# An average pooling kernel: stores of two tiles joined into one of 4 MiB, and the last row's store behind the section

## The chip, the cores and the metric

The kernel runs on one core of a Trainium2 chip. The metric is the device time of one execution in microseconds, the median of several runs; lower is better.

## What is computed

`x` has the shape (64, 256, 8192) in float32. Each of its 16,384 rows is cut into windows of four neighbours, and each window gives its mean:

```python
for i in range(out_len):
    start = i * stride            # kernel_size = stride = 4
    output[:, :, i] = np.mean(x[:, :, start : start + kernel_size], axis=2)
```

The output has 16,384 rows of 2,048. So 536.9 MB are read and 134.2 MB are written, and each output element takes three additions and one multiplication.

## The kernel before, in words

The rows are taken 256 at a time. Such a tile has two rows in each of the 128 partitions: 64 KiB per partition, 8 MiB in all, contiguous in memory. There are 64 tiles (`NT`). The input buffer `xin` has room for two of them (`_NIN`), the result buffer `res` for the results of four (`_NOUT`), 2 MiB each.

Four engines' programs are written out by hand inside a critical section (L58), each with its own loop, and tied by semaphores:

- **SP** issues the loads (`load`, L65 to L72). The first two go out at once. Each later one waits on `s_dve` until DVE has finished the tile that held its buffer two tiles earlier. The last tile is loaded as two halves of 4 MiB, one row of each partition each.
- **DVE** (`add_up`, L89 to L101) waits until the store that used the result slot four tiles earlier has landed (`s_out`) and until its tile has landed (`s_in`). It adds neighbours in place (`xin<-xin`, 8192 sums per partition), waits for that, and adds neighbours of the sums into `res` (`res<-xin`, 4096). Then `s_dve` goes up.
- **ACT** multiplies the result by 1/4 in place (`scale` L103, and L141 in the loop) and issues its store of 2 MiB (L143), whose packets have 16 KiB: two output rows of a partition.
- The stores of the last tiles are issued by SP behind its last loads (L119 to L121), except that of the last tile's first half, which ACT issues (L149). A second critical section (L153) waits for the stores.

Each of SP and ACT has a DMA ring of its own. In the profile SP's is q1 and ACT's is q10. A DMA of 128 partitions is cut into one packet per partition, 8 on each of the 16 DMA engines, and a packet of 4 bytes on each engine for the semaphore.

The loop counts: `U = _NOUT` tiles make one turn of a loop, `E = NT // U - 1` turns are in the loops, and the last four tiles are written out behind them.

Of the kernel before, what the change touches and what calls it, by code (L numbers as in the profile page):

```python
# [1 line left out]

# [4 lines left out]

_R = 2  # L10

_NIN = 2
_NOUT = 4


@with_exitstack
def kernel(
    ctx: ExitStack,
    tc: tile.TileContext,
    x: bass.AP,  # L20
    kernel_size: bass.AP,
    stride: bass.AP,
    out: bass.AP,
):
    nc = tc.nc
    K = int(kernel_size)
    assert K == int(stride) == 4
    P = nc.NUM_PARTITIONS
    dt = x.dtype
    inv_k = 1.0 / float(K)  # L30

    xf = x.flatten_outer_dims()
    of = out.flatten_outer_dims()
    rows, L = xf.shape
    OL = of.shape[1]
    R = _R
    T, OT = R * L, R * OL
    assert OL * K == L and rows % (P * R * _NOUT) == 0
    NT = rows // (P * R)

    xg = xf.rearrange("(t p r) m -> p t (r m)", p=P, r=R)
    og = of.rearrange("(t p r) m -> p t (r m)", p=P, r=R)

    pool = ctx.enter_context(tc.tile_pool(name="buf", bufs=1))
    xin = pool.tile([P, _NIN * T], dt)
    res = pool.tile([P, _NOUT * OT], dt)

    s_in = [tc.alloc_semaphore(f"s_in{b}") for b in range(_NIN)]  # L50
    s_out = [tc.alloc_semaphore(f"s_out{b}") for b in range(_NOUT)]
    s_dve = tc.alloc_semaphore("s_dve")
    s_act = tc.alloc_semaphore("s_act")
    s_half = tc.alloc_semaphore("s_half")
    s_last = tc.alloc_semaphore("s_last")
    s_fin = tc.alloc_semaphore("s_fin")

    with tc.tile_critical():  # L58

        U = _NOUT
        E = NT // U - 1

        def load(h, u, r0=0, r1=R, wait=True):  # L65
            b = u % _NIN
            if wait:
                nc.sync.wait_ge(s_dve, h * U + (u - _NIN + 1))
            nc.sync.dma_start(  # L69
                out=xin[:, b * T + r0 * L : b * T + r1 * L],  # L70
                in_=xg[:, h * U + u, r0 * L : r1 * L],
            ).then_inc(s_last if r0 > 0 else s_in[b], 16)  # L72

        def obuf(u, r0=0, r1=R):
            return res[:, u * OT + r0 * OL : u * OT + r1 * OL]

        def store(eng, h, u, r0=0, r1=R, again=False):
            eng.wait_ge(s_act, h * U + (u + 1 + (r1 - 1 if r1 - r0 < R else 0)))
            eng.dma_start(
                out=og[:, h * U + u, r0 * OL : r1 * OL], in_=obuf(u, r0, r1)  # L80
            ).then_inc(s_out[u] if again else s_fin, 16)

        def pairs(out, src):
            v = src.rearrange("p (m k) -> p m k", k=2)
            return nc.vector.tensor_tensor(  # L85
                out=out, in0=v[:, :, 0], in1=v[:, :, 1], op=mybir.AluOpType.add
            )

        def add_up(h, u, r0=0, r1=R):  # L89

            b = u % _NIN
            if r0 > 0:
                nc.vector.wait_ge(s_last, 16)
            else:
                nc.vector.wait_ge(s_out[u], h * 16)
                nc.vector.wait_ge(s_in[b], h * (U // _NIN * 16) + (u // _NIN + 1) * 16)  # L96
            src = xin[:, b * T + r0 * L : b * T + r1 * L]
            half = src[:, : (r1 - r0) * L // 2]
            pairs(half, src).then_inc(s_half, 1)
            nc.vector.wait_ge(s_half, h * U + (u + 1 + (r0 > 0)))  # L100
            pairs(obuf(u, r0, r1), half).then_inc(s_dve, 1)  # L101

        def scale(h, u, r0=0, r1=R):  # L103
            nc.scalar.wait_ge(s_dve, h * U + (u + 1 + (r0 > 0)))
            o = obuf(u, r0, r1)
            nc.scalar.mul(o, o, inv_k).then_inc(s_act, 1)  # L106

        for u in range(_NIN):  # L110
            load(0, u, wait=False)
        with nc.sync.Fori(0, E) as h:
            for u in range(_NIN, U + _NIN):
                load(h, u)
        for u in range(_NIN, U - 1):
            load(E, u)
        for r in range(R):
            load(E, U - 1, r, r + 1, wait=r == 0)
        for u in range(1, U - 1):  # L119
            store(nc.sync, E, u)  # L120
        store(nc.sync, E, U - 1, R - 1, R)  # L121


        with nc.vector.Fori(0, E) as h:
            for u in range(U):
                add_up(h, u)
        for u in range(U - 1):
            add_up(E, u)
        for r in range(R):
            add_up(E, U - 1, r, r + 1)  # L130

        scale(0, 0)
        nc.scalar.wait_ge(s_dve, 2)
        store(nc.scalar, 0, 0, again=True)
        with nc.scalar.Fori(0, E) as h:
            for u in range(1, U + 1):
                v = u % U
                nc.scalar.wait_ge(s_dve, h * U + (u + 1))  # L140
                nc.scalar.mul(obuf(v), obuf(v), inv_k).then_inc(s_act, 1)  # L141
                nc.scalar.wait_ge(s_act, h * U + (u + 1))
                nc.scalar.dma_start(out=og[:, h * U + u, :], in_=obuf(v)).then_inc(  # L143
                    s_out[v], 16
                )
        scale(E, 1)
        scale(E, 2)
        scale(E, 3, 0, 1)
        store(nc.scalar, E, 3, 0, 1)  # L149
        scale(E, 3, 1, 2)  # L150


    with tc.tile_critical():  # L153
        nc.sync.wait_ge(s_out[0], E * 16 + 16)
        nc.sync.wait_ge(s_fin, 64)


# [1 line left out]
_INS = ['x', 'kernel_size', 'stride']  # L159
_OUTS = [((64, 256, 2048), 'float32')]  # L160

_NUMBERS = {'kernel_size': 4, 'stride': 4}


# [26 lines left out]
```

## Time and profile before

| | |
|---|---|
| median of 5 runs | 1555.51 us (1555.32 to 1555.64) |
| profiled execution, its own time | 1555.71 us |
| its span | 1553.9 us |
| DVE busy | 839.8 us, 130 instructions |
| ACT busy | 232.9 us, 66 instructions |
| DMA | 671.10 MB, 18720 packets, mean 432 GB/s |

The span goes from the first to the last instruction of the profiled execution; 1.8 us of its time lie around it. The slices of DMA use on the profile's page are at 90% or more in all 40 slices. Under "waits", DVE waits for loads (702.8 us in 65 waits), ACT for DVE (1312.9 us in 65), and SP for DVE to free a buffer (1462.6 us in 62). Such waits are idle time of an engine; they cost something only where that engine is what the end waits for.

### The profile page before, as it was taken

What the parts mean: (1) busy time and instruction counts of PE and PEld (TensorE: products, weight loads), DVE (VectorE), ACT (ScalarE), POOL (GpSimd) and SP (SyncE); (2) the same over time, 40 slices, a digit from 0 to 9 for tenths busy, and PEclk for the clock granted to TensorE, in tenths of its full rate; (3) what the DMA queues carried; (4) which work ended last, traced back from release to release, by engine and by line L of the source; (5) the groups of instructions that cost most, each with busy time, mean ns of one, the idle gap of its engine ahead of it and who ended that gap; (6) DMA issues with size and microseconds to landing.
All of it is one profiled execution on the core that took longest, in us unless ns stands there. A gap on an engine that the chain in (4) does not pass through costs nothing.

```text
span 1553.9 us, 982 instructions
## 1 busy us (share of the span) xinstructions
DVE 839.8 (54%) x130; ACT 232.9 (15%) x66; POOL 0.2 (0%) x4
## 2 busy tenths in 40 slices
DVE  3645546456464564654646546455464554645546
ACT  1111011110111101111011010110111101111011
POOL 0000000000000000000000000000000000000000
DMA  9999999999999999999999999999999999999999
GB/s 408 420 434 439 439 439 434 420 445 422 439 439 437 434 417 435 437 439 432 442 433 419 434 435 442 439 434 430 424 434 439 439 439 434 423 430 434 439 428 402
DMA packets 18720, 671.10 MB, mean 432 GB/s; under 512 B 2080, under 2 KB 2080, under 8 KB 2080
## 3 DMA queue, kind: packets, MB, share of 16 engines
q1 hardware_dynamic: 9792, 542.12, 80.6%
q10 hardware_dynamic: 8928, 128.98, 19.4%
HBM read 536.87 MB, written 134.22 MB: 432 GB/s over the span
## 4 chain that ended last, share of the span: by engine, by line
DMA 72%; DVE 27%; issue 0%; SPq 0%; ACT 0%; DVEq 0%
DMA xin<-in_x_dram 72%; DVE xin L85 18%; DVE res L85 9%; SPq L69 0%; ACT res L106 0%; DVEq L96 0%; SPq L186 0%; SPq L58 0%
## 5 line engine op out<-in xcount | busy, mean ns | idle before, releaser
L85 DVE TENSOR_TENSOR xin<-xin 128x8192 f32<-128x8192 f32 (+1 forms) x65 | 556.5, 8561 | 702.8 <-DMA xin<-in_x_dram 702.8
L141 ACT ACTIVATE res<-res 128x4096 f32<-128x4096 f32 x60 | 217.0, 3616 | 1226.2 <-DVE res L85 1226.2
L85 DVE TENSOR_TENSOR res<-xin 128x4096 f32<-128x4096 f32 (+1 forms) x65 | 283.4, 4359 | 2.2
L106 ACT ACTIVATE res<-res 128x4096 f32<-128x4096 f32 (+1 forms) x5 | 14.7, 2934 | 86.7 <-DVE res L85 86.7
L106 ACT ACT_TABLE_LOAD x1 | 1.3, 1283 | 0.9 <-SPq L58 0.9
L172 POOL MEMSET const-bfloat16-1.0<- 128x1 bf16 x1 | 0.1, 101 | 0.0
L172 POOL MEMSET const-uint8-127<- 128x1 uint8 x1 | 0.1, 101 | 0.0
L172 POOL MEMSET const-float32-0.0<- 128x1 f32 x1 | 0.1, 98 | 0.2 <-issue 0.2
L172 POOL MEMSET const-float32-1.0<- 128x1 f32 x1 | 0.1, 98 | 0.0
## 6 DMA issues: line engine op xcount, KB each, us to landing
out_dram<-res ACTq DMA_DIRECT2D x61, 2048.0 KB, 52.4
xin<-in_x_dram SPq DMA_DIRECT2D x2, 4096.0 KB, 29.5
out_dram<-res SPq DMA_DIRECT2D x2, 2048.0 KB, 27.1
out_dram<-res ACTq DMA_DIRECT2D x1, 1024.0 KB, 13.1
out_dram<-res SPq DMA_DIRECT2D x1, 1024.0 KB, 5.9
xin<-in_x_dram SPq DMA_DIRECT2D x63, 34.9
```

The source lines that it names most:

```text
L85: return nc.vector.tensor_tensor(out=out, in0=v[:, :, 0], in1=v[:, :, 1], op=mybir.AluOpType.add)
L106: nc.scalar.mul(o, o, inv_k).then_inc(s_act, 1)
L141: nc.scalar.mul(obuf(v), obuf(v), inv_k).then_inc(s_act, 1)
L172: nc = _bacc.Bacc("TRN2", target_bir_lowering=False, num_devices=1)
```

## The change

It has these parts:

- A group of four rows per partition (`_F = 4`) takes the place of the tile as the unit of layout. A tile is still two rows per partition and 8 MiB, but two tiles now make one group of 16 MiB, and a tile's 64 KiB in a partition are half of the 128 KiB that the group has there.
- `res` has two slots of 4 MiB (`_NOUT = 2`), one for each group of results. ACT scales both tiles of a group and then issues one store of 4 MiB with packets of 32 KiB. DVE waits for a slot's store once per group.
- DVE works on a whole tile in four instructions: the pair sums of the first 8,704 inputs in place (4352), their pair sums into `res` (2176), the pair sums of the other 7,680 inputs into a new buffer `hb` (3840, `_B`), and their pair sums into `res` (1920). After the third the input buffer is free, and `s_free`, which loads wait for, goes up there.
- At the end ACT issues no late stores. SP issues, behind its loads, one store of 4 MiB and one of 3 MiB (three of four rows), and behind the critical section, as soon as that is left, the last row's 1 MiB. The section waits for no late store; there is no second section.

Cut to its core:

```diff
-_NOUT = 4
+_F = 4
+_NOUT = 2
+_B = 3840
...
-    og = of.rearrange("(t p r) m -> p t (r m)", p=P, r=R)
+    og = of.rearrange("(g p f) m -> p g (f m)", p=P, f=F)
+    xg = xf.rearrange("(g p f) m -> p g (f m)", p=P, f=F)
...
-    res = pool.tile([P, _NOUT * OT], dt)
+    res = pool.tile([P, _NOUT * F * OL], dt)
+    hb = pool.tile([P, _B], dt)
...
-        U = _NOUT
+        U = _NOUT * G
...
-                nc.sync.wait_ge(s_dve, h * U + (u - _NIN + 1))
+                nc.sync.wait_ge(s_free, h * U + (u - _NIN + 1))
...
+            if u % G == 0 and r0 == 0:
+                nc.vector.wait_ge(s_out[u // G], h * 16)
...
-            pairs(half, src).then_inc(s_half, 1)
+            n = (r1 - r0) * L // 2
+            a = n if r1 - r0 < R else n - _B
+            o = obuf(u, r0, r1)
+            pairs(src[:, :a], src[:, : 2 * a]).then_inc(s_half, 1)
             nc.vector.wait_ge(s_half, h * U + (u + 1 + (r0 > 0)))
-            pairs(obuf(u, r0, r1), half).then_inc(s_dve, 1)
+            last = pairs(o[:, : a // 2], src[:, :a])
+            if a < n:
+                pairs(hb[:, :], src[:, 2 * a :]).then_inc(s_free, 1)
+                nc.vector.wait_ge(s_free, h * U + (u + 1))
+                last = pairs(o[:, a // 2 :], hb[:, :])
+            last.then_inc(s_dve, 1)
...
-        for u in range(1, U - 1):
-            store(nc.sync, E, u)
-        store(nc.sync, E, U - 1, R - 1, R)
+        store(nc.sync, E, _NOUT - 2, NT - G)
+        store(nc.sync, E, _NOUT - 1, NT - 1 + R - 1, F - 1)
...
         with nc.scalar.Fori(0, E) as h:
+            for u in range(U):
+                scale(h, u)
+                if u % G == G - 1:
+                    store(nc.scalar, h, u // G, h * U + (u + 1))
+        for u in range(U - 1):
+            scale(E, u)
+        for r in range(R):
+            scale(E, U - 1, r, r + 1)
+        nc.sync.wait_ge(s_out[_NOUT - 1], E * 16)
...
-    with tc.tile_critical():
-        nc.sync.wait_ge(s_out[0], E * 16 + 16)
-        nc.sync.wait_ge(s_fin, 64)
+    nc.sync.dma_start(
+        out=og[:, NG - 1, (F - 1) * OL :], in_=res[:, (_NOUT * F - 1) * OL :]
+    )
```

Here `G = F // R = 2` is the number of tiles in a group, and `store` moves the first `f1` rows of a slot (all four, or three).

## The prediction

> **What bounds the kernel now.** I read the page's share of busy time first, then the DMA figures, then the chain of waits, then the instructions in order of time for one tile, and last the packet records of the trace.
>
> ```profile
> span 1553.9 us, 982 instructions
> DVE 839.8 (54%) x130; ACT 232.9 (15%) x66; POOL 0.2 (0%) x4
> DMA packets 18720, 671.10 MB, mean 432 GB/s; under 512 B 2080, under 2 KB 2080, under 8 KB 2080
> q1 hardware_dynamic: 9792, 542.12, 80.6%
> q10 hardware_dynamic: 8928, 128.98, 19.4%
> DMA 72%; DVE 27%; issue 0%; SPq 0%; ACT 0%; DVEq 0%
> ```
>
> No engine is busy for more than 54%, while the two DMA queues together take 80.6% + 19.4% = 100% of the 16 DMA engines. The chain, with 27% on DVE, seems to say otherwise: load, then DVE, then the next load into the same buffer. One tile in order of time shows why this is no bound:
>
> ```profile
> 1189.27 24.57 SPq L69 DMA_DIRECT2D xin<-in_x_dram  x2
> 1192.89 0.34 ACTq L143 DMA_DIRECT2D out_dram<-res  x1
> 1200.17 8.69 DVE L85 TENSOR_TENSOR xin<-xin 128x8192 f32<-128x8192 f32 x1 [11.10 <-DMA xin<-in_x_dram]
> 1208.90 4.43 DVE L85 TENSOR_TENSOR res<-xin 128x4096 f32<-128x4096 f32 x1
> 1213.36 3.62 ACT L141 ACTIVATE res<-res 128x4096 f32<-128x4096 f32 x1 [20.64 <-DVE res L85]
> 1217.15 0.34 ACTq L143 DMA_DIRECT2D out_dram<-res  x1
> 1224.30 8.69 DVE L85 TENSOR_TENSOR xin<-xin 128x8192 f32<-128x8192 f32 x1 [10.97 <-DMA xin<-in_x_dram]
> ```
>
> A load is issued at 1189.27 and the tile before it lands only at 1200.1 (DVE starts at 1200.17). So its descriptors lie in the ring 10.9 us before their turn; the 34.9 us "to landing" are 10.9 us of queueing and 24.1 us of transfer. Between landings there are 24.18 us, of which DVE works 13.1 and idles 11. Per step 8 MiB + 2 MiB = 10.486 MB move: 433.7 GB/s. Integrating the packet records, I find that from 64 us to 1551 us the engines lose about 0.05 us against back-to-back packets. The 6.3 us of the span that are not packets: 2.0 before the first packet, 0.85 in the first packets, 1.1 around 58 to 62 us when the store ring starts, 1.0 while the engines run out and 1.2 after the last store lands.
>
> [...] a 64 KiB load packet, then a 16 KiB store packet, so a store lands 52.4 us after issue although it is 4.8 us of work. [...]
>
> **The cost of a packet, from the trace.** In the load-only stretch from 16 to 35 us consecutive 64 KiB packets of an engine start 2,414 ns apart (each recorded as 2,418 long, so they overlap by 4). A semaphore packet of 4 bytes delays its successor by 6 ns. A steady step is (1490.35 - 136.20)/56 = 24.181 us between DVE starts, for 8 load packets, 8 store packets and 2 semaphore packets on each engine: (24,181 - 12)/8 - 2,414 = 607 ns for 16 KiB. Four of those would be 2,428 for the bytes of one 64 KiB packet: 14 ns more for three more packets, so 4.8 ns each. The raw durations give an upper bound: 2 x 611 - 1,213 (32 KiB packets, the halves of the last tile) = 9 ns.
>
> **The change part by part.**
> *Stores of 4 MiB.* Store packets per engine before: 63 x 8 of 16 KiB + 16 of 8 KiB = 520. After: 15 x 2 + 1 stores with 8 of 32 KiB, then 8 of 24 KiB and 8 of 8 KiB = 264. Saved: 256 x 4.8 = 1.2 us, all of it on the bound. DMAs fall from 130 to 65 + 33 = 98: 32 x 6 ns = 0.2 us. Bounds: 0 and 256 x 9 + 32 x 9 = 2.6 us.
> *New mix.* A 4 MiB store has 8 packets on each engine, as one load has, so store and load alternate through one load (about 29 us) and the next load runs alone (19.3). The sum is the same if the rate does not depend on the mix. The trace shows load only, 4:1, 2:1 (the last two 4 MiB loads in 32 KiB packets beside 16 KiB stores, 1514 to 1526 us) and store only (1540 on) without lost time. I take nothing.
> *Addresses.* A load now takes 64 KiB of every 128 KiB per partition, where it took adjacent 64 KiB. The last tile of before takes 32 KiB of every 64 and its packets run at the usual 1,213 ns, so I take nothing; price unknown upwards (rival C).
> *DVE in four pieces.* From 8192, 4096 and 2048 elements (8,692, 4,425, 2,292 ns): 158 ns + 1.042 ns per element. 4352, 2176, 3840 and 1920 give 4.69 + 2.43 + 4.16 + 2.16 = 13.43 us instead of 13.12: +0.32 per tile, 20 us in all, beside the DMA in 11 us of idle. At the shortest landing distance (some 19 to 20 us) there are still 6 us of cover; were that gone, 0.3 per tile would show. The buffer is free after the third, at about 11.3 us instead of 13.1, so a load lies 1.8 us longer in the ring. That costs and gains nothing, because the ring is never empty: landings are at least 19.3 us apart, and the load that then takes over was issued 11.3 us after the landing before, so 8 us ahead of its turn.
> *Two result slots.* DVE waits for the store of two groups ago. It is issued 17.2 us after an odd tile landed and needs 29 plus some 2 us: landed by about 49. The slot is wanted 20 + 28 + 20 = 68 us after that landing: 19 us spare. Queued behind that DVE wait would be both adds and with them the next load.
> *Tail.* All late stores are on SP, behind all loads in ring 1. No store is left on ACT by then, so after the last load 8 MiB of stores follow (19.3 us) where 6 MiB did; that landing (L) comes about as much earlier. The 4 MiB store is ready long before L. The 3 MiB one needs the first half of the last tile: landed L-9.7, DVE busy with the tile before until L-6, then 6.7 + 1.9: issued at L+3, wanted at L+9.7. The last MiB: DVE until L+7.5, ACT L+9.5, exit of the section about 0.7 us (1546.8 to 1547.5 in before), issue at L+10.3; before, ACT's late store needed 3.5 us from issue to first packet, so L+14, wanted at L+16.9. Spare: 3 us. DMA is fed to the end, cost nothing; if the cover is gone, the miss adds one to one. Waiting for the section's end lets SP hold only this one store, and nobody waits behind it.
> *End.* One critical section less after the last landing: its NOPs lie between 1552.8 and 1553.1, so -0.2 (0 to -0.4).
>
> Sum: -1.2 - 0.2 - 0.2 = -1.6. The profiled execution took 1555.71 around its span of 1553.9; new span 1552.3. Its time lies 0.2 above the median of 1555.51, which I use: 1555.5 - 1.6 = 1553.9.
>
> **Rivals.** A, as costed: 1553.9; with bounds 1552.5 to 1555.6.
> B, slower: the ACT ring runs empty after each store and each start stalls the engines. When the ring first started, one load packet on each engine took 3.4 to 3.75 us instead of 2.42: 1.06 us lost. Before, the ring is then full until 1526.8 us, so the price is paid once; now it would be paid 31 times: + 30 x 1.06 = 32 us, 1587. Against it: in before the ring is empty from 1526.8 to 1540.7 and restarts with no lost time, though beside SP's stores and not loads. It decides against the forecast from 0.16 us per restart (30 x 0.16 = 4.8, less 1.6, is 0.2%).
> C, slower: the doubled row distance in HBM slows reads. [...]
> D, faster by more than the costed: packets cost the full 9 ns and the end saves 0.4: -3.0; with a first-store stall of 1.1 that vanishes: 1551.5.
> E, the chain taken at its word: earlier buffers cut 1.8 us from every second tile, 58 us, 1498. But 671.1 MB in 1498 us is 448 GB/s, above anything sustained here: excluded.
>
> **Chances.** A 0.76, B 0.10, C 0.07, D 0.06, others on the slow side (a late last store) 0.01. About 0.2%, 3.1 us, is what a measurement of this kernel can tell from no change: faster 0.06, same 0.76, slower 0.18. The range goes from 1551.4 (D) to 1560, which takes in a restart of up to (1560 - 1553.9)/30 = 0.2 us.
>
> **What would show it.** 14112 packets, 1568 under 512 B; GB/s 433 to 434 throughout; DVE x256 near 860 us; landings alternately about 20 and 28 us apart, 48.3 in pairs; the last landing near 1531; no DVE wait for a store. Wrong: load packets over 2.42 us at every store's start (B) or everywhere (C), or a gap before the last MiB.

## The result, and the profile after

| | before | after |
|---|---|---|
| median | 1555.44 us (42 runs, 1555.06 to 1555.89) | 1566.17 us (22 runs, 1553.95 to 1571.81) |
| profiled execution: its time, its span | 1555.71, 1553.9 us | 1572.45, 1570.7 us |

The ratio of the means is 1.0054, with an interval of 1.004 to 1.0068: slower, by more than the 0.2% that the prediction took as the least that can be told. The spread is as much of a result as the median: the kernel before stays within 0.9 us, the changed one spreads over 18 us. Its fastest run, 1553.95, is the forecast of 1553.9, and 5 of the 22 runs lie within 1 us of it; 14 runs are 11 to 18 us above it.

The page of the changed kernel:

```profile
span 1570.7 us, 991 instructions
DVE 853.9 (54%) x256; ACT 250.9 (16%) x80; POOL 0.2 (0%) x4
GB/s 426 414 426 437 427 424 431 426 428 431 427 434 430 431 429 424 431 429 438 429 426 423 433 434 427 424 420 425 437 429 423 431 428 427 427 436 432 430 427 380
DMA packets 14112, 671.09 MB, mean 427 GB/s; under 512 B 1568, under 2 KB 1568, under 8 KB 1568
q1 hardware_dynamic: 9792, 545.26, 81.2%
q10 hardware_dynamic: 4320, 125.83, 18.6%
DMA 75%; DVE 24%; issue 0%; SPq 0%; ACT 0%; DVEq 0%
```

The packets fell to 14112, as counted, and the two queues still fill the DMA engines (81.2% + 18.6%). Yet they move 427 GB/s instead of 432. So the engines are busy with packets that take longer, and the share of busy time does not show it; the GB/s do. The last of the 40 slices has 380 GB/s where before had 402: some of the 16 engines end earlier than others (in the packet records the last packet of an engine ends between 1564.4 and 1569.5 us, and between 1551.4 and 1552.3 us in the trace of before). The same line of before:

```profile
GB/s 408 420 434 439 439 439 434 420 445 422 439 439 437 434 417 435 437 439 432 442 433 419 434 435 442 439 434 430 424 434 439 439 439 434 423 430 434 439 428 402
```

The order of time around one store, in the changed kernel (start, duration, engine, line):

```profile
1219.38 4.69 DVE L99 TENSOR_TENSOR xin<-xin 128x4352 f32<-128x4352 f32 x1 [16.32 <-DMA xin<-in_x_dram]
1232.82 3.62 ACT L132 ACTIVATE res<-res 128x4096 f32<-128x4096 f32 x1 [26.11 <-DVE res L99]
1236.60 0.34 ACTq L92 DMA_DIRECT2D out_dram<-res  x1
1238.73 4.69 DVE L99 TENSOR_TENSOR xin<-xin 128x4352 f32<-128x4352 f32 x1 [5.94 <-DMA xin<-in_x_dram]
```

The store is issued 17.2 us after DVE has started on the odd tile (1219.38), which it does as soon as that has landed, and 2 us later the next tile has landed (1238.73). The packet records of the trace, one start and one duration for each packet, say what follows: the store's first packets move from 1240.1 on, and between 1238 and 1245 most engines have a 64 KiB load packet that takes 2.5 to 3.4 us instead of 2.418. This is called a stall below, and what a packet takes beyond the usual time its excess. Nearly every store in the loop has such packets at its start. Between 100 and 1500 us the excess is 15.8 us as a mean over the engines, 0.55 us for each of the 29 starts (single starts: 0.08 to 1.04). It is uneven, so the engines drift apart: around 1200 us a load's first engine is done 5 to 9 us before its last one.

### The profile page after: what moved, and what is told of

Its sections match the earlier page's. It is cut to its first block, busy times and chain, and to the rows that moved or that the text cites. A ratio compares the mean times of both kernels' runs of the same rounds, so it can differ in the third digit from the quotient of the medians.

```text
span 1570.7 us, 991 instructions
## 1 busy us (share of the span) xinstructions
DVE 853.9 (54%) x256; ACT 250.9 (16%) x80; POOL 0.2 (0%) x4
## 2 busy tenths in 40 slices
DMA packets 14112, 671.09 MB, mean 427 GB/s; under 512 B 1568, under 2 KB 1568, under 8 KB 1568
## 3 DMA queue, kind: packets, MB, share of 16 engines
q1 hardware_dynamic: 9792, 545.26, 81.2%
q10 hardware_dynamic: 4320, 125.83, 18.6%
## 4 chain that ended last, share of the span: by engine, by line
DMA 75%; DVE 24%; issue 0%; SPq 0%; ACT 0%; DVEq 0%
DMA xin<-in_x_dram 75%; DVE xin L99 10%; DVE hb L99 8%; DVE res L99 5%; SPq L81 0%; ACT res L132 0%; DVEq L115 0%; SPq L205 0%; SPq L69 0%
## 5 line engine op out<-in xcount | busy, mean ns | idle before, releaser
L99 DVE TENSOR_TENSOR xin<-xin 128x4352 f32<-128x4352 f32 (+1 forms) x65 | 304.5, 4684 | 699.6 <-DMA xin<-in_x_dram 699.6
L132 ACT ACTIVATE res<-res 128x4096 f32<-128x4096 f32 (+1 forms) x65 | 231.6, 3564 | 1296.1 <-DVE res L99 1296.1
L99 DVE TENSOR_TENSOR hb<-xin 128x3840 f32<-128x3840 f32 x63 | 261.5, 4151 | 0.0
L99 DVE TENSOR_TENSOR res<-xin 128x2176 f32<-128x2176 f32 (+1 forms) x65 | 157.4, 2421 | 2.2
L99 DVE TENSOR_TENSOR res<-hb 128x1920 f32<-128x1920 f32 x63 | 135.9, 2158 | 2.2
```

The costliest lines, as they stand in the source:

```text
L99: return nc.vector.tensor_tensor(out=out, in0=v[:, :, 0], in1=v[:, :, 1], op=mybir.AluOpType.add)
```

## The experiments

The kernel before ran beside every version, with medians between 1555.33 and 1555.39, so medians are compared directly and the ratio is given where it decides. "Even" means runs within about 2 us of each other.

My first theory was R, rival B of the prediction: a store that starts in an emptied ring stalls the engines. Its rivals were L, the new addresses, and W, the change from reading alone to reading and writing.

**e1_after_again: the changed kernel once more.** No edit.

> The changed kernel once more, unaltered, for the spread of its own times and a second trace. Theory R (each start of the emptied ACT ring stalls load packets, by an amount that differs from execution to execution): times again between 1554 and 1572, and every loss in the trace lies within some 4 us of a store's issue; the loss per store, times 30, is what the span is above 1552.3. Theory L (the new addresses of loads and stores, 64 KiB of every 128 KiB): losses also lie far from any store's issue.

Median 1568.5, from 1554.27 to 1579.04. In the profiled execution the loss stops halfway. Two stretches of that one trace (length, busy time of DVE, ACT and POOL, clock, DMA share, GB/s):

```profile
100.00:700.00 600.00, 326.48 (x99) 99.38 (x32) 0.00 (x0) 1.00 1.00 430
750.00:1500.00 750.00, 411.23 (x124) 121.08 (x38) 0.00 (x0) 1.00 1.00 434
```

The reader is to see 430 and 434 GB/s at the same DMA share of 1.00. In the packet records the starts from 100 to 603 us cost 0.4 to 0.7 us each and none from 749 us on more than 0.1, though the ring is empty before each of them, the instructions are the same and the store's first packet moves 1.7 to 2.0 us after a landing in both parts. So a start in an emptied ring need not cost anything: theory R lacks a condition.

**e2_one_ring: stores by SP, in the loads' ring.**

```diff
                 load(h, u)
+                if u % G == G - 1:
+                    store(nc.sync, h, u // G - 1, h * U + (u - 1))
...
                 scale(h, u)
-                if u % G == G - 1:
-                    store(nc.scalar, h, u // G, h * U + (u + 1))
```

> The changed kernel with every store issued by SP, behind the second load that it issues in the same half turn, so that loads and stores lie in one ring that never runs empty; sizes, packets and addresses as in the changed kernel. Theory R: no stalls, every execution within 1 us of 1553.9. Theory L: 1554 to 1572 as before. Theory W (each change from reads of HBM alone to reads and writes costs, whatever the ring): the stall stays at each store, 1560 or more.

1558.10, 1557.68 to 1559.65: even, but 4 us above what R said. One ring carries everything:

```profile
q1 hardware_dynamic: 14112, 671.09, 99.9%
```

The packet records show small stalls, 2.6 us in all after the first two, nearly all before 520 us, where stores follow loads. So passing from loads to stores of 32 KiB packets can cost even without a second ring; most of the changed kernel's loss is gone with it.

**e3_before_ring_empties: the kernel before with 32 KiB load packets.**

```diff
-            nc.sync.dma_start(
-                out=xin[:, b * T + r0 * L : b * T + r1 * L],
-                in_=xg[:, h * U + u, r0 * L : r1 * L],
-            ).then_inc(s_last if r0 > 0 else s_in[b], 16)
+            for r in range(r0, r1):
+                nc.sync.dma_start(
+                    out=xin[:, b * T + r * L : b * T + (r + 1) * L],
+                    in_=xg[:, h * U + u, r * L : (r + 1) * L],
+                ).then_inc(s_last if r0 > 0 else s_in[b], 16)
```

> The kernel before, with each load of 8 MiB issued as two of 4 MiB with packets of 32 KiB, so that a store of 16 KiB packets is served in about 12 us of each 24 us step and the ACT ring runs empty 62 times; stores and addresses of the store as in before. More packets cost 504 x 4.8 ns and 63 x 6 ns = 2.8 us. Theory R: 62 x 0.5 us more, about 1590 (at least 1570), and uneven. Theory L, or packets of 32 KiB in the store: 1558.

1559.56, even. Its page shows that the ring did empty: a store lands 18.4 us after its issue, and one is issued every 24.3.

```profile
out_dram<-res ACTq DMA_DIRECT2D x61, 2048.0 KB, 18.4
```

Some 60 starts in an emptied ring cost 0.01 us each. Theory R in its simple form has fallen. (In the packet records these starts lie 3.2 us ahead of a landing; e12 moves them.) The time is that of the packets: 2.8 us were worked out for them, 4.2 measured.

**e4_before_group_rows: the kernel before with the rows of the changed one.**

```diff
-    xg = xf.rearrange("(t p r) m -> p t (r m)", p=P, r=R)
-    og = of.rearrange("(t p r) m -> p t (r m)", p=P, r=R)
+    xg = xf.rearrange("(g p f) m -> p g (f m)", p=P, f=F)
+    og = of.rearrange("(g p f) m -> p g (f m)", p=P, f=F)
```

> The kernel before with only the rows dealt out as in the changed kernel (four rows per partition and group, a tile is half of a group): stores still 2 MiB per tile with packets of 16 KiB and a ring that is never empty. Theory R: 1555.5, even. Theory L: 1556 to 1572, uneven.

1555.31, even; ratio 0.9999 (0.9991 to 1.0007). Theory L has fallen: the layout costs nothing.

Two things remained: the size of the store's packets (theory P), and the moment of its start (theory C: it meets the boundary at which the engines pass from one load to the next).

**e5_two_stores_of_16k: the same 4 MiB by two DMAs.**

```diff
-            eng.dma_start(
-                out=og[:, h * _NOUT + j, : f1 * OL],
-                in_=res[:, j * F * OL : (j * F + f1) * OL],
-            ).then_inc(s_out[j], 16)
+            for f in range(0, f1, R):
+                e = min(f + R, f1)
+                eng.dma_start(
+                    out=og[:, h * _NOUT + j, f * OL : e * OL],
+                    in_=res[:, (j * F + f) * OL : (j * F + e) * OL],
+                ).then_inc(s_out[j], 16)
```

> The changed kernel, with each group's 4 MiB stored by two DMAs of 2 MiB at the same moment, so that the packets have 16 KiB again and the mix with the loads is 4 to 1; all else as in the changed kernel. Theory P (stalls come from 32 KiB store packets beside 64 KiB load packets): none but the first, every execution near 1555.4 (1553.9 plus 256 packets of 4.8 ns and 32 semaphores of 6 ns). Theory R (a store that meets an emptied ring, of whatever packets): the ring is now busy for about 45 of 48 us and still starts anew 30 times, so 1558 to 1572 and uneven.

1555.44, even, as theory P said. With this mix the store is served as slowly as it is filled, and its ring has no gap over 2.3 us in the records, so the run does not tell packets apart from an occupied ring. It shows something else. DVE now waits for stores:

```profile
DVE xin L101 <- DMA out_dram<-res: 399.0, 30, 13.8
DVE xin L101 <- DMA xin<-in_x_dram: 284.4, 33, 22.9
```

399 us of waiting in 30 waits cost nothing that shows in the time: the DMA engines are busy for 90% or more in all 40 slices of the page, at a mean of 432 GB/s.

**e6_loads_of_32k: loads in halves.** The edit is that of e3, in the changed kernel.

> The changed kernel, with each 8 MiB load issued as two DMAs of 4 MiB, so that loads too have packets of 32 KiB; the 4 MiB stores of 32 KiB packets stay and are served in 19 us. More packets cost 504 x 4.8 ns and 63 x 6 ns = 2.8 us. Theory P: if 32 KiB in the store is enough, 1560 to 1575 and uneven; if it takes the pair with a 64 KiB load, even at 1556.7. Theory R: 1560 to 1575.

1562.24; four of six runs within 1561.17 to 1562.41, two at 1570.93 and 1572.84. Halving the load packets alone does not cure it. Its stores start 1.6 to 2.1 us after a landing. In the profiled execution, one of the four shorter runs, the stalls are only 1.3 us and nearly all before 600 us, as in e1, but the engines drift apart by up to 7.8 us, and the last one sets the end.

**e7_store_7us_later: two multiplications ahead of the scaling.**

```diff
+                if u % G == G - 1:
+                    nc.scalar.wait_ge(s_dve, h * U + (u + 1))
+                    o = obuf(u)
+                    nc.scalar.mul(o, o, 0.5).then_inc(s_mid, 1)
+                    nc.scalar.wait_ge(s_mid, h * U + u)
+                    nc.scalar.mul(o, o, 2.0).then_inc(s_mid, 1)
+                    nc.scalar.wait_ge(s_mid, h * U + (u + 1))
                 scale(h, u)
```

> The changed kernel with two more multiplications (by 0.5 and by 2) of the odd tile's results on ACT ahead of the scaling, so that each store in the loop is issued 7.5 us later; the results are the same. In the changed kernel a store's first packets move about 20.7 us after the odd tile's landing, within 2 us of the next load's first packets (19.3 us). Theory C (that meeting makes the stall): even, 1553.9. Theory R or P: 1554 to 1575, uneven as before.

1554.39, from 1554.13 to 1554.58. ACT does 30 x 2 more instructions of 3.6 us, and the kernel becomes even and 12 us faster than the changed one. The ring is empty before each start as before. In its order of time a store's issue now lies behind the landing of the next tile:

```profile
1174.63 4.69 DVE L100 TENSOR_TENSOR xin<-xin 128x4352 f32<-128x4352 f32 x1 [8.36 <-DMA xin<-in_x_dram]
1177.38 0.34 ACTq L93 DMA_DIRECT2D out_dram<-res  x1
```

The moment matters.

**e8_table_load_once: the activation table ahead of the loop.**

```diff
+        nc.scalar.mul(one[:, :], one[:, :], inv_k)
         with nc.scalar.Fori(0, E) as h:
```

> The changed kernel with one tiny activation ahead of ACT's loop, so that the activation table is loaded once and not 15 times in the loop, as the changed kernel's page shows. Theory T (the table loads, each right behind a store's issue, make the stalls): even, 1553.9. All other theories: 1554 to 1575, uneven, since stores without a table load behind them stalled as well.

The changed kernel's page has the first of these lines, this version's page the second:

```profile
L132 ACT ACT_TABLE_LOAD x15 | 19.2, 1283 | 12.8 <-ACT res L132 11.8
```

```profile
L160 ACT ACT_TABLE_LOAD x1 | 1.3, 1283 | 1.1 <-SPq L71 1.1
```

1564.80, 1554.61 to 1572.22: uneven as before. The 15 loads of the table, which I had not seen coming, are not what makes the stalls; e7 has them too and is even.

**e9, e10 and e11: other moments.** e9 multiplies one row by 1.0 ahead of the scaling, e10 both rows (the lines of e7 with one multiplication). e11 leaves out the scaling by 1/4 of every second tile in the loop.

> The changed kernel with one more multiplication (by 1.0, of one of the two rows) on ACT ahead of the odd tile's scaling: each store in the loop is issued 1.9 us later, so that its first packets move some 22.6 us after the odd tile's landing, 3.3 us after the next load's first ones. Theory C (a store that starts within some 2 to 5 us of the boundary of two loads stalls): still uneven, but less than the changed kernel, 1554 to 1568. Theory B (the stall comes with any start that is not as late as 7 us): 1554 to 1575 as in the changed kernel.

> As the one before, with both rows multiplied by 1.0: the store is issued 3.7 us later, 24.4 us after the landing, 5.1 us after the boundary. Theory C: nearly even, 1554 to 1557. Theory B: 1554 to 1575.

> The changed kernel without the scaling by 1/4 of every second tile in the loop, so that its store is issued right after DVE's sums, 3.6 us earlier: the first packets move 17.1 us after the landing, 2.2 us ahead of the boundary of two loads. Theory C, if only a start behind the boundary stalls: even, 1554. If the boundary that passes while the store runs in stalls as well: uneven, 1554 to 1572.

1580.04, 1570.35 and 1554.88. Here neither C nor its rival had the sizes right: 2 us later is the worst, not better. Put together by the moment at which the store's first packet moves, counted from the nearest landing of a tile (packet records of one profiled execution each, 100 to 1500 us; the first column is the median of 29 starts):

| first packet, us after the landing | kernel | mean excess per start, us | median of its runs, us |
|---|---|---|---|
| -3.0 | e11 | 0.01 | 1554.88 |
| 1.9 | changed kernel | 0.55 | 1566.17 |
| 3.2 | e9 | 0.69 | 1580.04 |
| 4.4 | e10 | 0.41 | 1570.35 |
| 6.7 | e7 | 0.01 | 1554.39 |
| 9.2 | e16 | 0.01 | 1554.66 |

So a store of this kind that starts 1.9 to 4.4 us behind a landing stalls the loads, and one that starts 3 us ahead of it, or 6.7 us or more behind it, does not (0.01 us per start). The edges lie somewhere between these moments; no run looked for them. In e9 the store is issued when the next tile lands:

```profile
1191.42 0.34 ACTq L93 DMA_DIRECT2D out_dram<-res  x1
1191.59 4.69 DVE L100 TENSOR_TENSOR xin<-xin 128x4352 f32<-128x4352 f32 x1 [5.93 <-DMA xin<-in_x_dram]
```

Its stretches show that the price of such a start is not fixed even within one execution: in the packet records e9's starts cost 0.17 us in the mean up to 700 us and 1.11 from 750 us on, and the GB/s fall with it:

```profile
100.00:700.00 600.00, 327.03 (x99) 124.20 (x45) 0.00 (x0) 1.00 1.00 433
750.00:1500.00 750.00, 407.50 (x123) 146.10 (x52) 0.00 (x0) 1.00 1.00 424
```

**e12_before_empties_and_meets: e3 at the bad moment.**

```diff
                 nc.scalar.wait_ge(s_act, h * U + (u + 1))
+                nc.scalar.mul(obuf(v), obuf(v), 1.0).then_inc(s_mid, 1)
+                nc.scalar.wait_ge(s_mid, h * 2 * U + (2 * u - 1))
+                nc.scalar.mul(obuf(v, 0, 1), obuf(v, 0, 1), 1.0).then_inc(s_mid, 1)
+                nc.scalar.wait_ge(s_mid, h * 2 * U + (2 * u))
```

> The kernel before with 32 KiB load packets, whose ring of stores runs empty in each step and which was even at 1559.6, now with 5.6 us more of ACT's multiplications by 1.0 ahead of each store, so that a store of 16 KiB packets starts about 2 us after a boundary of two loads. Theory C alone (the meeting is enough): uneven, 1565 to 1600. If it takes the 32 KiB packets of the changed kernel's stores besides: even, 1559.6.

1559.82, even. Its stores start 2.3 us after a landing, in an emptied ring, and cost 0.01 us each. So the moment alone is not enough either: with packets of 16 KiB in the store and 32 KiB in the load a start there costs nothing (one moment was tried).

**e13 and e14: what the store meets.** Both start from e9. e13 has 20 tiny activations behind each store, and DVE waits for them:

```diff
+                    for i in range(20):
+                        m = nc.scalar.mul(tiny[:, :], tiny[:, :], 1.0)
...
+                nc.vector.wait_ge(s_go, h * _NOUT + u // G)
```

> The kernel with stores 1.9 us later (1580 us), and besides 20 tiny activations on ACT behind each store, for which DVE waits before it begins the tile that has just landed: DVE starts some 7.5 us after that landing and not at once, while the store starts 3.3 us after it as before. Theory D (the stall comes from DVE's first sums working while the store starts): even, 1554 to 1556. Theory Q (the stall arises among the DMA's own packets): 1576 to 1590.

1573.82, from 1568.42 to 1577.36. In order of time in e13, a store's issue and the first sums of the tile that has landed:

```profile
1185.12 0.34 ACTq L97 DMA_DIRECT2D out_dram<-res  x1
1193.49 4.69 DVE L104 TENSOR_TENSOR xin<-xin 128x4352 f32<-128x4352 f32 x1 [14.14 <-ACT tiny L176]
```

DVE idles for 14 us around the store's start, and the stalls stay (0.34 us per start). Theory D has fallen as the cause. The 6 us less than e9 have two candidates, DVE's absence and a start 0.7 us nearer to the landing (2.5 instead of 3.2); they were not separated.

```diff
+    sh = 3 * F
+    os = of[sh : sh + (NG - 1) * P * F, :].rearrange("(g p f) m -> p g (f m)", p=P, f=F)
...
-                out=og[:, h * _NOUT + j, : f1 * OL],
+                out=(os if eng is nc.scalar else og)[:, h * _NOUT + j, : f1 * OL],
```

> The kernel with stores 1.9 us later (1580 us), with the stores in the loop writing 12 rows (96 KiB) further on, so that loads and stores that meet have other addresses relative to each other; the results of the loop so lie 12 rows too far. Theory A (reads and writes of HBM that collide by their addresses): another time, by 5 us or more either way. All others: 1576 to 1582.

The stores of e14's loop write 12 rows (96 KiB) further on, so its results lie there; besides, SP waits for the loop's last store before it issues the late ones.

1580.61: as e9. At least this shift of the addresses changes nothing.

**e15_16k_at_the_worst: e5 with e9's multiplication.**

> The kernel with two stores of 2 MiB and 16 KiB packets (even at 1555.4), its stores 1.9 us later, at the moment that was worst for 32 KiB packets. Theory P2 (the moment matters only for 32 KiB packets): even, 1555.4. If the moment matters for all: 1565 to 1580.

1555.52, even. As in e5 the ring hardly runs empty (no gap over 4.5 us in the records), so this confirms a safe version more than a cause.

**e16_store_waits_for_sums: the moment without idle work.**

```diff
                 if u % G == G - 1:
+                    nc.scalar.wait_ge(s_half, h * U + (u + 2))
                     store(nc.scalar, h, u // G, h * U + (u + 1))
```

> The changed kernel with each store in the loop waiting until DVE has done the first sums of the next tile (4.7 us after its landing): the store is issued some 7 us later than in the changed kernel, without idle work on ACT. All theories that rest on the moment: even, 1553.9 to 1554.5, below the kernel before (1555.4).

1554.66, from 1554.44 to 1554.97. Its page and, below, its order of time:

```profile
span 1552.7 us, 1036 instructions
DMA packets 14112, 671.09 MB, mean 432 GB/s; under 512 B 1568, under 2 KB 1568, under 8 KB 1568
```

```profile
1199.97 4.69 DVE L99 TENSOR_TENSOR xin<-xin 128x4352 f32<-128x4352 f32 x1 [12.13 <-DMA xin<-in_x_dram]
1222.80 4.69 DVE L99 TENSOR_TENSOR xin<-xin 128x4352 f32<-128x4352 f32 x1 [9.41 <-DMA xin<-in_x_dram]
1227.66 0.34 ACTq L92 DMA_DIRECT2D out_dram<-res  x1
1248.25 4.69 DVE L99 TENSOR_TENSOR xin<-xin 128x4352 f32<-128x4352 f32 x1 [12.04 <-DMA xin<-in_x_dram]
```

The store is issued 4.9 us after DVE has started on a landed tile, and two landings take 48.3 us. With the packets of the changed kernel, this one wait brings the mean back to 432 GB/s. The span of the changed kernel, 1570.7 us, is 18.0 us longer than this one; 15.8 us of that are the excess of its load packets, and the rest is put down to the drift, since the last engine sets the end.

**e17 and e18: the boundary.** Was it the boundary of two loads, which passes at the landing? In e18 the scaling of the odd tile, too, stands behind e16's wait; e17 besides cuts the odd tile's load into two DMAs of 64 partitions:

```diff
+            parts = 2 if b == 1 and r1 - r0 == R else 1
+            n = P // parts
+            for k in range(parts):
+                nc.sync.dma_start(
+                    out=xin[k * n : (k + 1) * n, b * T + r0 * L : b * T + r1 * L],
```

> The kernel whose store waits for the next tile's first sums, with ACT's scaling of the odd tile behind that wait too, so that the store starts some 12 us after the landing (31.4 us after the odd tile's); and each odd tile's load issued as two DMAs of 64 partitions, packets of 64 KiB as before, so that a boundary of two loads passes 9.7 us after that landing, 2 to 3 us ahead of the store. Theory C (the boundary is what the store meets): uneven, 1565 to 1580. If not the boundary but the time since a whole tile's landing counts: even, 1554 to 1555.

> The same with the odd tile's load in one DMA: the store starts some 12 us after the landing and after the only boundary. All theories: even, 1554 to 1555.

e18: 1554.54, even. e17: five of its seven runs lie between 2266.48 and 2294.73 (median 2268.03), the other two at 2432 and 2454; what sets those two apart was not shown. The page is that of the longest:

```profile
span 2451.9 us, 1127 instructions
DMA packets 14608, 671.10 MB, mean 274 GB/s; under 512 B 2064, under 2 KB 2064, under 8 KB 2064
```

64 KiB load packets took 3.9 us in the mean in that execution, where 2.418 us are usual elsewhere. Why loads cut into two DMAs of 64 partitions are slower was not shown. With the loads themselves that slow, e17 says nothing on the boundary.

The kept traces say something on it. They do not name a packet's engine, but packets of one engine follow each other without a gap (in the traces of before and of the changed kernel each starts within 0.06 us of the end of the one ahead), so nearly all can be put into 16 chains, and for each engine one can read how long before the store's first packet it passed its own boundary of two loads. Where that was 8.8 to 11.5 us, 185 of 240 engines stalled in e9 (a load packet over 0.25 us too long), 1 of 217 in e7 and none of 441 in e16. So an engine's own boundary does not decide whether it stalls: in e9 the early engines stall though theirs is long past. What sets e9 apart is that its last engines had passed theirs, and the tile had landed, only some 3 us before; which of the two counts is open.

## Why the prediction was wrong

**What bounds the kernel** was right: both queues fill the engines (together 99.8% of their time in the changed kernel, 99.9% in e1 and e2; e17, at 274 GB/s, is a case apart), and earlier buffers or 399 us of DVE waits (e5) change nothing.

**Stores of 4 MiB, the packets saved.** Right in sign and rough in size. The cleanest pair is e5 and e18, which differ in the packets and in the moment: 1555.44 - 1554.54 = 0.9 us, where 1.4 were worked out. e5 itself stands 0.05 us above the kernel before (1555.39), so layout, DVE's four pieces, the new tail and the section's end together bring nothing that can be told; 0.2 us for the end is less than the intervals resolve. Without the stalls the sum was right to within 0.5 to 0.8 us: 1553.9 against 1554.39 (e7) to 1554.66 (e16).

**New mix: this step failed.** The prediction said that "the sum is the same if the rate does not depend on the mix", found every mix in the trace of before at full speed, and took nothing. Each steady mix is indeed at full speed: e16, which has both, moves 434 GB/s from 100 to 700 us and from 750 to 1500 us, where before moves 433. What failed is the step from steady mixes to nothing at all: the change from one mix to the other, 30 times in the loop, was put at 0. The trace of before does not contain such a start of a store of 32 KiB packets beside 64 KiB loads, a few us behind a landing: its loop never lets the ring run empty (a store lands 52.4 us after its issue, and the next is issued after 24.2). In the changed kernel it costs 0.55 us in the mean, 15.8 us from 100 to 1500 us, and with the drift of the engines 18 us of span.

**Rival B** named the place, but its reason, the emptied ring, was not sufficient: e3, e7, e11, e12, e16 and e18 all start in an emptied ring at 0.01 us. That its price, 1.06 us per start, was of the order of the 0.55 measured is luck. It was read from the first store of the execution, and that one stalls the loads in every trace with a ring for stores except e17: by 0.6 to 1.3 us as a mean over the engines, with 16 KiB and with 32 KiB packets, from 9 us ahead of a landing to 10 us behind one. e7, e16 and e18 pay it once, at 1.0 to 1.1 us, and next to nothing afterwards. So it does not wait for the moment that the later starts need. For the same reason the first stall did not vanish, as rival D supposed: the changed kernel pays 0.8 us. I gave B one chance in ten because one restart at 1540.7 us had cost nothing. That restart had 8 KiB packets and, as the prediction itself says, no loads beside it: it was not the case to be judged. The range to 1560 allowed for 0.2 us per start.

**Rivals C and E** are settled: the layout costs nothing (e4: 1555.31 us, and 1555.33 for the kernel before beside it), and earlier buffers gain nothing (e18: 1554.54, where E had 1498).

**DVE in four pieces, two slots, tail**: DVE took 853.9 us in 256 instructions (near 860 were forecast) and never waited for a store. The last MiB was issued at 1560.01 us in the changed kernel, while the 3 MiB store ahead of it landed at 1567.4: the ring was fed. One sum in the prediction is off, with nothing resting on it: its parts of the 6.3 us of span that are not packets add up to 6.15.

**What stays open.** Shown is that behind the first store a start stalls the loads only at certain moments, that in the one pairing of smaller packets tried there (e12) it does not, and that the cause is not the ring's emptiness alone, not the layout, not the table loads and not DVE's sums. Not shown is what in the DMA engines or in HBM makes it. The boundary of the last engine was not tested apart from the landing (e17), and one shift of addresses only (e14). The moment is not sufficient: the same start costs nothing from the middle of e1's trace on, and over six times as much in the later part of e9's as in the earlier one; neither is explained, nor is the stall of the first store. And store packets of 32 KiB and load packets of 64 KiB were not told apart fully: 32 with 32 loses less in most runs (e6), 16 with 32 nothing (e12).

**A better version.** e7, e16 and e18 lie below the kernel before in every run (at most 1554.97 against at least 1555.13 in the runs beside e16), by 0.7 to 1.0 us. The intervals of the ratios are wider than that: e7 0.9993 (0.9985 to 1.0001), e16 0.9995 (0.9987 to 1.0004). It is at best 0.07%.

## What to carry to other kernels

When the DMA engines are the bound, look at GB/s and packet durations and not at the busy share: a stalled packet counts as busy (a share of 1.00 at 424 and at 434 GB/s here). A change that lets a transfer queue run empty creates starts that the old trace does not contain; judge such a start by one with the same packets and the same traffic beside it, and not by the first of the execution, or leave it in the range at its full price. If a kernel's times spread by 1%, try moving the issue of one DMA by a few microseconds before anything else is redesigned.

## What the runs showed of the hardware

A store of 32 KiB packets that started 1.9 to 4.4 us behind a tile's landing stretched 64 KiB load packets on most engines from 2.418 to as much as 4.4 us (e9); started 3 us ahead of the landing or 6.7 us behind it, it did not (0.01 us per start in e11 and e7). The stalls are uneven over the engines, whose ends of one load then drifted apart by up to 9 us (changed kernel) and 11 us (e9), and the slowest sets the end (in the changed kernel the engines' last packets end from 1564.4 to 1569.5 us of a span of 1570.7). In the same program the stalls can stop for good in the middle of an execution (e1: 0.4 to 0.7 us per start up to 603 us, none over 0.1 from 749 us on). The first store of an execution stalled the loads by 0.6 to 1.3 us at whatever moment it came. Cutting every second load into two of 64 partitions, with packets of 64 KiB as before, took the whole kernel from 1554.5 to 2268 us.
